# A weight-gradient matmul: slice 1 moved from the hardware queues to the casting queue, and a warm-up without a gap

## The chip, the cores and the metric

One core of a Trainium2 chip runs the kernel. The metric is the device time of one execution in microseconds (us). A time given for a kernel is the median of several executions. The granted TensorE clock was between 0.997 and 1.0 in all but two. Those two are executions of the kernel before, 179.28 and 179.5 us at a clock of 0.99, in two later series (e1 to e4 and e9 to e12); they stand almost 2 us above all its others and no cause is known. I compare medians. The ratios of those eight runs in the table below still contain them, which lowers these ratios by about 0.001 and widens their intervals.

## The reference

```python
# input (16, 512, 1024) f32, grad_output (16, 512, 768) f32
grad_weight = np.einsum('bmk,bmn->kn', input, grad_output)   # (1024, 768) f32
```

It is one matmul that contracts over 16 x 512 = 8192 rows. The kernel cuts them into 64 *slices* of 128 rows. A slice reads 128 x (1024 + 768) x 4 B = 0.92 MB.

## The kernel before

Each slice gives twelve 512-column bf16 matmuls in three *groups* of four: A (output rows 0 to 511, columns 0 to 511), B (output rows 512 to 1023, the same columns) and N (the other 256 columns, transposed). A group that is open holds four of the eight PSUM banks, so only two of the three can be open at once. `ORDER` says in which order the groups are worked off: `B12!` means "B, up to and with slice 11, then close", and closing adds the four banks to sums in SBUF, by VectorE. The queues of SyncE and ScalarE are called the hardware queues here, and that of GpSimd, which rounds f32 to bf16 on the way, the casting queue. In the cuts of code `...` stands for what is left out, and the comments are mine.

```python
ORDER = (
    "A1! N1 B2! N2 A2 N3! A3 B3 A4! B5 N5 B6! N7 A6 N8! A9! B10 N9 B12! N12! A12! "
    "B15 A15 AB16 A19! B19! N19! A22 B22 AB28 A31! B31! N31! A34 B34 AB47 A50! B50! N64!"
).split()
HW = 2
WARMUP = 9
...
# slices 0 and 1 in f32 over the queues of SyncE and ScalarE; other engines round them
nc.sync.dma_start(out=gf[0], in_=G[rows[0], 0:NA])
nc.scalar.dma_start(out=xf[0][:, 0:NA], in_=X[rows[0], 0:NA])
nc.sync.dma_start(out=gnf, in_=G[rows[0], NA:N])
nc.scalar.dma_start(out=xf[0][:, NA:K], in_=X[rows[0], NA:K])
nc.sync.dma_start(out=gf[1], in_=G[rows[1], 0:NA])
nc.scalar.dma_start(out=xf[1], in_=X[rows[1], :])
...
for i in range(WARMUP):
    nc.tensor.matmul(wps, ones, ones_wide, start=(i == 0), stop=(i == WARMUP - 1))
...
nc.gpsimd.dma_start(out=gn1, in_=G[rows[1], NA:N])
for s in range(HW, S):                      # 62 slices cast to bf16 by the transfer itself
    ...
    nc.gpsimd.dma_start(out=gt, in_=G[s * P : (s + 1) * P, :])
    nc.gpsimd.dma_start(out=xt, in_=X[s * P : (s + 1) * P, :])
```

After `ORDER`, slices 50 to 63 of A and B are worked off one output row block after the other, so that stores can start; this last stretch has a fixed length.

Of the kernel before, what the change touches and what calls it, by code (L numbers as in the profile page):

```python
# [8 lines left out]
P = 128  # L9
NA = 512  # L10
# [7 lines left out]
    "B15 A15 AB16 A19! B19! N19! A22 B22 AB28 A31! B31! N31! A34 B34 AB47 A50! B50! N64!"  # L18
).split()

HW = 2
WARMUP = 9
XBUFS = 42


# [1 line left out]
def kernel(  # L27
# [6 lines left out]
    nc = tc.nc  # L34
    bf16 = mybir.dt.bfloat16
    f32 = mybir.dt.float32

    B, M, K = input.shape
    _, _, N = grad_output.shape
    S = B * M // P  # L40
    KS = K // P
    NB = N - NA
# [3 lines left out]
    X = input.rearrange("b m k -> (b m) k")  # L46
    G = grad_output.rearrange("b m n -> (b m) n")
    OUT = out.rearrange("(ks p) n -> p ks n", p=P)

    head = ctx.enter_context(tc.tile_pool(name="head", bufs=1))  # L50
# [11 lines left out]
    xs = [None] * S  # L62
    gwide = [None] * S
    gnarrow = [None] * S
# [1 line left out]
    E = mybir.EngineType  # L66
    ctx.enter_context(tc.manual_schedule(engines={E.PE, E.DVE, E.Activation}))

    xf = [head.tile([P, K], f32, name=f"xf{s}") for s in range(HW)]
    gf = [head.tile([P, NA], f32, name=f"gf{s}") for s in range(HW)]  # L70
    gnf = head.tile([P, NB], f32, name="gnf")
    rows = [slice(s * P, (s + 1) * P) for s in range(HW)]
    nc.sync.dma_start(out=gf[0], in_=G[rows[0], 0:NA])
    nc.scalar.dma_start(out=xf[0][:, 0:NA], in_=X[rows[0], 0:NA])  # L74
    nc.sync.dma_start(out=gnf, in_=G[rows[0], NA:N])
    nc.scalar.dma_start(out=xf[0][:, NA:K], in_=X[rows[0], NA:K])  # L76
    nc.sync.dma_start(out=gf[1], in_=G[rows[1], 0:NA])
    nc.scalar.dma_start(out=xf[1], in_=X[rows[1], :])


    ones = nc.const_aps.tensor(1.0, (P, P), bf16)
    ones_wide = nc.const_aps.tensor(1.0, (P, NA), bf16)
    wps = psum.tile([P, NA], f32, name="bank7")
    for i in range(WARMUP):
        nc.tensor.matmul(wps, ones, ones_wide, start=(i == 0), stop=(i == WARMUP - 1))  # L85


    gn1 = head.tile([P, NB], bf16, name="gn1")
    nc.gpsimd.dma_start(out=gn1, in_=G[rows[1], NA:N])
    gnarrow[1] = gn1  # L90
    for s in range(HW, S):
        gt = xg.tile([P, N], bf16, name="gt")
        xt = xg.tile([P, K], bf16, name="xt")
        nc.gpsimd.dma_start(out=gt, in_=G[s * P : (s + 1) * P, :])  # L94
        nc.gpsimd.dma_start(out=xt, in_=X[s * P : (s + 1) * P, :])  # L95
        xs[s] = xt
        gwide[s] = gt[:, 0:NA]
        gnarrow[s] = gt[:, NA:N]

    QX = 256  # L100

    def round_pair(dst, src, c):
        nc.vector.tensor_copy(out=dst[:, c : c + QX], in_=src[:, c : c + QX])  # L103
        nc.scalar.copy(out=dst[:, c + QX : c + 2 * QX], in_=src[:, c + QX : c + 2 * QX])  # L104

    def round_slice(s):
        gt = head.tile([P, NA], bf16, name=f"g{s}")
        xt = head.tile([P, K], bf16, name=f"x{s}")
        round_pair(gt, gf[s], 0)

        for c in (0, NA) if s == 0 else (NA, 0):
            round_pair(xt, xf[s], c)
            if s == 0 and c == 0:
                gn0 = head.tile([P, NB], bf16, name="gn0")
                nc.vector.tensor_copy(out=gn0, in_=gnf)
                gnarrow[0] = gn0
        xs[s] = xt
        gwide[s] = gt

    def add_out(dst, src):  # L120
        nc.vector.tensor_add(out=dst, in0=src, in1=dst)  # L121

    def copy_out(dst, src, i):
        if i % 2 == 0:
            nc.vector.tensor_copy(out=dst, in_=src)  # L125
        else:
            nc.scalar.copy(out=dst, in_=src)  # L127

    def wide_mm(bank, k, s, start, stop, c0=0, c1=NA):
        nc.tensor.matmul(  # L130
            bank, xs[s][:, k * P : (k + 1) * P], gwide[s][:, c0:c1], start=start, stop=stop
        )
# [30 lines left out]
    def one_slice(part, close):  # L163
        s = part.done
        part.done += 1
        if s < HW and xs[s] is None:
            round_slice(s)
        opened = part.banks is None
        if opened:
            names = [free.pop(0) for _ in part.groups]  # L170
            part.banks = [(name, psum.tile([P, NA], f32, name=name)) for name in names]
        for i, (group, (name, bank)) in enumerate(zip(part.groups, part.banks)):
            part.matmul(bank, *group, s, opened, close)
            if close:
                dst = part.dst(*group)
                if part.first:
                    copy_out(dst, bank, i)
                else:
                    add_out(dst, bank)
                if part is parts["N"] and s == S - 1:  # L180
                    t, h = group
                    hb = NA // SQ
                    nc.vector.transpose(  # L183
                        out=turned[:, h * hb : (h + 1) * hb, :, t],
                        in_=dst.rearrange("p (b r) -> p b r", r=SQ),
                    )
                free.append(name)
        if close:
            part.banks = None
            part.first = False  # L190

    for step in ORDER:
        close = step.endswith("!")
        names = step.rstrip("!").rstrip("0123456789")
        upto = int(step.strip("ABN!"))
        while any(parts[n].done < upto for n in names):
            for n in names:
                if parts[n].done < upto:
                    one_slice(parts[n], close and parts[n].done == upto - 1)

    rows_of = out.rearrange("(b r) n -> r b n", r=SQ)
    for a in range(P // SQ):
        c = NA + a * NT * SQ
        nc.scalar.dma_start(
            out=rows_of[:, :, c : c + NT * SQ],
            in_=turned[a * SQ : (a + 1) * SQ].rearrange("p b r t -> p b (r t)"),
# [3 lines left out]
    for k in range(KS):  # L210
        slices = range(parts["A" if k < KS // 2 else "B"].done, S)
        pieces = [(0, NA)] if k < KS - 1 else [(0, 256), (256, 384), (384, NA)]
        for c0, c1 in pieces:
            name = free.pop(0)
            bank = psum.tile([P, NA], f32, name=name)[:, 0 : c1 - c0]
            for s in slices:
                wide_mm(bank, k, s, s == slices[0], s == slices[-1], c0, c1)
            add_out(acc[:, k, c0:c1], bank)
            free.append(name)
            W = NB if k < 4 else c1 - c0  # L220
            for c in range(c0, c1, W):
                nc.sync.dma_start(out=OUT[:, k, c : c + W], in_=acc[:, k, c : c + W])

# [29 lines left out]
```

## Time and profile before

| | kernel before |
|---|---|
| time | 177.08 us, 3 runs (176.94 to 177.35) |
| span in the profile | 175.2 us |
| TensorE busy | 171.0 us, 98% |
| DMA engines | full from about 4 to 144 us |
| matmuls | 768 of 512 columns at 0.216 us = 165.9 us, plus a slow start |

The prediction shows the page's busy rows, the pieces of the chain (the work that ended last, followed back from the last instruction; start, length, what) and the timeline of the start (start, busy time, engine, line, operation, count; in brackets the idle time before it and what ended it). Two more lines matter later. Here is one from the pieces of the chain (start, length, what):

```profile
35.02 14.73 PE bank L130 x68
```

And one from the timeline of the weight loads between 44 and 51 us (start, busy time, engine, line, operation, count; in brackets the idle time before it and what ended it):

```profile
46.13 3.13 PEld L130 LDWEIGHTS <-xt 128*128 128x128 bf16 x16 [0.38 <-DMA xt<-in_input_dram]
```

The first says that from 35.0 to 49.8 us TensorE works off A and B groups alone. The second says that at 46.13 us a weight load, which normally runs ahead of its matmul, had to wait for a slice that had only just landed. TensorE itself hardly stood still there: the matmul began 0.05 us late.

### The profile page before, as it was taken

How to read it: one execution, taken by the hardware profiler on the slowest of the kernel's cores; microseconds unless marked ns; L12 is line 12 of the kernel's file. 1: busy time of each engine (PE TensorE's matmuls, PEld its weight loads, DVE VectorE, ACT ScalarE, POOL GpSimd, SP SyncE). 2: the span in 40 equal slices, each digit the busy share in tenths (PEclk: the TensorE clock that was granted, in tenths of full speed). 3: DMA queues.
4: the chain of work that ended last, by engine and by line, in shares of the span. 5: the costliest groups of instructions: out<-in, count | busy, mean ns of one | idle time of the engine just before them, and what ended most of it. 6: DMA issues, size and time to landing. Idle time of an engine off the chain costs nothing.

```text
span 175.2 us, 1999 instructions
## 1 busy us (share of the span) xinstructions
PE 171.0 (98%) x805; PEld 77.8 (44%) x805; DVE 54.0 (31%) x91; ACT 6.8 (4%) x13; POOL 66.3 (38%) x129
## 2 busy tenths in 40 slices
PE   8999999999999999999999999999999999999993
PEld 2244444444444444444444444444444444444463
DVE  0665564790374100280320000047000003932122
ACT  3650000000000000000000000000000000000000
POOL 7344443444444444444444444444274200000000
PEclk9999999999999999999999999999999999999999
DMA  5999999999999999999999999999999990087513
GB/s 168 313 209 209 209 208 206 208 210 209 207 212 204 209 208 209 208 208 209 208 209 208 209 207 209 208 208 208 208 208 209 207 188 4 0 182 196 164 60 120
DMA packets 25048, 33.48 MB, mean 191 GB/s; under 512 B 6480, under 2 KB 16080, under 8 KB 25040
## 3 DMA queue, kind: packets, MB, share of 16 engines
q0 software_dynamic: 18000, 28.52, 89.0%
q1 hardware_dynamic: 2448, 2.75, 4.7%
q10 hardware_dynamic: 4592, 2.10, 4.6%
q8 instruction: 6, 0.10, 0.2%
q14 instruction: 2, 0.02, 0.0%
HBM read 58.72 MB, written 3.15 MB: 353 GB/s over the span
## 4 chain that ended last, share of the span: by engine, by line
PE 93%; DMA 4%; ACTq 0%; DVE 0%; issue 0%
PE bank L130 62%; PE bank L137 31%; DMA xf<-in_input_dram 4%; ACTq L76 0%; ACTq L74 0%; DVE x L103 0%; DVE acc L121 0%
## 5 line engine op out<-in xcount | busy, mean ns | idle before, releaser
L130 PE MATMUL bank<-gt,xt 128*128 128x512 bf16 (+2 forms) x524 | 108.7, 368 | 0.0
L130 PEld LDWEIGHTS <-xt 128*128 128x128 bf16 x524 | 50.0, 98 | 57.5 <-DMA xt<-in_input_dram 0.4
L121 DVE TENSOR_TENSOR acc<-bank,acc 128x512 f32<-128x512 f32 (+2 forms) x54 | 33.1, 664 | 71.7 <-PE bank L130 71.2
L137 PE MATMUL bank<-xt,gt 128*128 128x512 bf16 x248 | 55.0, 379 | 0.0
L95 POOL DMA_DIRECT2D xt<-in_input_dram x62 | 32.9, 530 | 36.1 <-DMA xt<-in_input_dram 35.4
L94 POOL DMA_DIRECT2D gt<-in_grad_output_dram x62 | 32.9, 531 | 33.9 <-DMA gt<-in_grad_output_dram 30.6
L137 PEld LDWEIGHTS <-gt 128*128 128x128 bf16 x248 | 24.3, 98 | 29.3
L121 DVE TENSOR_TENSOR acct<-bank,acct 128x512 f32<-128x512 f32 x20 | 12.6, 679 | 39.4 <-PE bank L137 39.3
L130 PE MATMUL bank<-g,x 128*128 128x512 bf16 x16 | 4.9, 438 | 0.6 <-DVE x L103 0.5
L85 PE MATMUL bank<-const-bfloat16-1.0 128*128 128x512 bf16 x9 | 4.0, 626 | 0.8 <-PEq L237 0.8
L130 PEld LDWEIGHTS <-x 128*128 128x128 bf16 x16 | 1.5, 106 | 3.8 <-DVE x L103 2.0
L183 DVE STREAM_TRANSPOSE turned<-acct 128x512 f32<-128x512 f32 x4 | 2.9, 714 | 0.1
L125 DVE COPY acc<-bank 128x512 f32<-128x512 f32 x4 | 2.7, 686 | 0.3 <-PE bank L130 0.3
L85 PEld LDWEIGHTS <-const-bfloat16-1.0 128*128 128x128 bf16 x9 | 1.2, 138 | 2.7 <-issue 2.7
L103 DVE CAST g<-gf 128x256 bf16<-128x256 f32 x2 | 0.6, 319 | 5.5 <-DMA gf<-in_grad_output_dram 5.5
L127 ACT COPY acc<-bank 128x512 f32<-128x512 f32 x4 | 2.2, 587 | 0.6 <-PE bank L130 0.5
L137 PE MATMUL bank<-x,gn 128*128 128x512 bf16 x8 | 2.1, 379 | 0.0
L125 DVE COPY acct<-bank 128x512 f32<-128x512 f32 x2 | 1.3, 686 | 1.3 <-PE bank L137 1.3
L104 ACT CAST x<-xf 128x256 bf16<-128x256 f32 x4 | 1.5, 402 | 0.5 <-DMA xf<-in_input_dram 0.5
L137 PEld LDWEIGHTS <-gn 128*128 128x128 bf16 x8 | 0.8, 105 | 1.2 <-issue 0.5
L104 ACT ACT_TABLE_LOAD x1 | 1.3, 1283 | 2.2 <-issue 2.2
L103 DVE CAST x<-xf 128x256 bf16<-128x256 f32 x4 | 1.1, 287 | 0.3 <-DMA xf<-in_input_dram 0.3
(8 smaller groups left out, 3.2 us busy)
## 6 DMA issues: line engine op xcount, KB each, us to landing
xt<-in_input_dram POOLq DMA_DIRECT2D x62, 256.0 KB, 8.5
gt<-in_grad_output_dram POOLq DMA_DIRECT2D x62, 192.0 KB, 8.5
out_dram<-acc SPq DMA_DIRECT2D x9, 128.0 KB, 2.9
out_dram<-turned ACTq DMA_DIRECT2D x4, 256.0 KB, 3.2
out_dram<-acc SPq DMA_DIRECT2D x3, 256.0 KB, 2.0
gf<-in_grad_output_dram SPq DMA_DIRECT2D x2, 256.0 KB, 5.1
xf<-in_input_dram ACTq DMA_DIRECT2D x2, 256.0 KB, 4.0
xf<-in_input_dram ACTq DMA_DIRECT2D x1, 512.0 KB, 6.9
```

The source lines that it names most:

```text
L85: nc.tensor.matmul(wps, ones, ones_wide, start=(i == 0), stop=(i == WARMUP - 1))
L94: nc.gpsimd.dma_start(out=gt, in_=G[s * P : (s + 1) * P, :])
L95: nc.gpsimd.dma_start(out=xt, in_=X[s * P : (s + 1) * P, :])
L103: nc.vector.tensor_copy(out=dst[:, c : c + QX], in_=src[:, c : c + QX])
L104: nc.scalar.copy(out=dst[:, c + QX : c + 2 * QX], in_=src[:, c + QX : c + 2 * QX])
L121: nc.vector.tensor_add(out=dst, in0=src, in1=dst)
L125: nc.vector.tensor_copy(out=dst, in_=src)
L127: nc.scalar.copy(out=dst, in_=src)
L130: nc.tensor.matmul(bank, xs[s][:, k * P : (k + 1) * P], gwide[s][:, c0:c1], start=start, stop=stop)
L137: nc.tensor.matmul(bank, gnarrow[s].rearrange("p (r t) -> p t r", t=NT)[:, t], xs[s][:, h * NA : (h + 1) * NA], start=start, stop=stop,)
L183: nc.vector.transpose(out=turned[:, h * hb : (h + 1) * hb, :, t], in_=dst.rearrange("p (b r) -> p b r", r=SQ),)
```

## The change

Its intent: give the hardware queues only slice 0, so that it is not followed by 0.79 MB of slice 1; let the casting queue of GpSimd round slice 1 on the way in, so that VectorE and ScalarE need not; keep TensorE's warm-up going until the data are there. Rows 4 and 5 of output blocks are also stored in two pieces instead of one. The diff is shortened; what stands in angle brackets, and the line of `round_pair`, are put together by me.

```diff
-HW = 2
-WARMUP = 9
+WARMUP = [512] * 9 + [128] * 3
...
-nc.sync.dma_start(out=gf[1], in_=G[rows[1], 0:NA])
-nc.scalar.dma_start(out=xf[1], in_=X[rows[1], :])
...
-for i in range(WARMUP):
-    nc.tensor.matmul(wps, ones, ones_wide, start=(i == 0), stop=(i == WARMUP - 1))
-gn1 = head.tile([P, NB], bf16, name="gn1")
-nc.gpsimd.dma_start(out=gn1, in_=G[rows[1], NA:N])
-for s in range(HW, S):
+for i, cols in enumerate(WARMUP):
+    nc.tensor.matmul(wps[:, 0:cols], ones, <ones, cols wide>, start=True, stop=True)
+for s in range(1, S):
     ... two GpSimd transfers per slice ...
...
-            round_slice(s)                  # casts of slices 0 and 1
+round_pair(g0, gf, 0); round_pair(xs[0], xf, 0); <cast of g0's narrow part>; round_pair(xs[0], xf, NA)
...
-            W = NB if k < 4 else c1 - c0
+            W = NB if k < 6 else c1 - c0
```

`ORDER` stays as it was.

More of the change, by code (lines that the diff above doesn't have):

```diff
@@ L67 @@
     ctx.enter_context(tc.manual_schedule(engines={E.PE, E.DVE, E.Activation}))
-    xf = [head.tile([P, K], f32, name=f"xf{s}") for s in range(HW)]
-    gf = [head.tile([P, NA], f32, name=f"gf{s}") for s in range(HW)]
-    gnf = head.tile([P, NB], f32, name="gnf")
-    rows = [slice(s * P, (s + 1) * P) for s in range(HW)]
-    nc.sync.dma_start(out=gf[0], in_=G[rows[0], 0:NA])
-    nc.scalar.dma_start(out=xf[0][:, 0:NA], in_=X[rows[0], 0:NA])
-    nc.sync.dma_start(out=gnf, in_=G[rows[0], NA:N])
-    nc.scalar.dma_start(out=xf[0][:, NA:K], in_=X[rows[0], NA:K])
-    nc.sync.dma_start(out=gf[1], in_=G[rows[1], 0:NA])
-    nc.scalar.dma_start(out=xf[1], in_=X[rows[1], :])
+    xf = head.tile([P, K], f32, name="xf")
+    gf = head.tile([P, N], f32, name="gf")
+    nc.sync.dma_start(out=gf[:, 0:NA], in_=G[0:P, 0:NA])
+    nc.scalar.dma_start(out=xf[:, 0:NA], in_=X[0:P, 0:NA])
+    nc.sync.dma_start(out=gf[:, NA:N], in_=G[0:P, NA:N])
+    nc.scalar.dma_start(out=xf[:, NA:K], in_=X[0:P, NA:K])
     ones = nc.const_aps.tensor(1.0, (P, P), bf16)
-    ones_wide = nc.const_aps.tensor(1.0, (P, NA), bf16)
     wps = psum.tile([P, NA], f32, name="bank7")
-    for i in range(WARMUP):
-        nc.tensor.matmul(wps, ones, ones_wide, start=(i == 0), stop=(i == WARMUP - 1))
-    gn1 = head.tile([P, NB], bf16, name="gn1")
-    nc.gpsimd.dma_start(out=gn1, in_=G[rows[1], NA:N])
-    gnarrow[1] = gn1
-    for s in range(HW, S):
+    for i, cols in enumerate(WARMUP):
+        nc.tensor.matmul(
+            wps[:, 0:cols],
+            ones,
+            nc.const_aps.tensor(1.0, (P, cols), bf16),
+            start=True,
+            stop=True,
+        )
+    for s in range(1, S):
         gt = xg.tile([P, N], bf16, name="gt")
@@ L98 @@
         gnarrow[s] = gt[:, NA:N]
+    xs[0] = head.tile([P, K], bf16, name="x0")
+    g0 = head.tile([P, N], bf16, name="g0")
+    gwide[0] = g0[:, 0:NA]
+    gnarrow[0] = g0[:, NA:N]
     QX = 256
@@ L104, in round_pair @@
         nc.scalar.copy(out=dst[:, c + QX : c + 2 * QX], in_=src[:, c + QX : c + 2 * QX])
-    def round_slice(s):
-        gt = head.tile([P, NA], bf16, name=f"g{s}")
-        xt = head.tile([P, K], bf16, name=f"x{s}")
-        round_pair(gt, gf[s], 0)
-        for c in (0, NA) if s == 0 else (NA, 0):
-            round_pair(xt, xf[s], c)
-            if s == 0 and c == 0:
-                gn0 = head.tile([P, NB], bf16, name="gn0")
-                nc.vector.tensor_copy(out=gn0, in_=gnf)
-                gnarrow[0] = gn0
-        xs[s] = xt
-        gwide[s] = gt
+    round_pair(g0, gf, 0)
+    round_pair(xs[0], xf, 0)
+    nc.vector.tensor_copy(out=g0[:, NA:N], in_=gf[:, NA:N])
+    round_pair(xs[0], xf, NA)
     def add_out(dst, src):
@@ L165, in one_slice @@
         part.done += 1
-        if s < HW and xs[s] is None:
-            round_slice(s)
         opened = part.banks is None
```

## The prediction

> **What bounds the kernel now.** I read the page's busy shares first, then the chain that ended last with its pieces in order of time, then the timeline of the first 12 us, since everything that the change touches but one store width lies there. The page:
>
> ```profile
> PE 171.0 (98%) x805; PEld 77.8 (44%) x805; DVE 54.0 (31%) x91; ACT 6.8 (4%) x13; POOL 66.3 (38%) x129
> ...
> DMA  5999999999999999999999999999999990087513
> GB/s 168 313 209 209 209 208 206 208 210 209 207 212 204 209 208 209 208 208 209 208 209 208 209 207 209 208 208 208 208 208 209 207 188 4 0 182 196 164 60 120
> ```
>
> TensorE is busy 98% of the span, and the DMA engines too are full, from the second slice to about 144 us. The pieces of the chain say where the matmuls stop being the limit:
>
> ```profile
> 1.67 6.91 DMA xf<-in_input_dram
> ...
> 8.60 0.31 DVE x L103
> ...
> 8.95 1.04 PE bank L130 x4
> 9.99 0.86 PE bank L137 x4
> 10.85 0.86 PE bank L130 x4
> ...
> 148.18 24.26 PE bank L130 x140
> 172.44 0.02 issue
> 172.46 0.29 DVE acc L121
> ```
>
> Four 512-column matmuls take 0.86 us, so one takes 0.216. There are 64 slices of 12 of them (768). Of these, 12 belong to slice 0 and come before 8.95 us; the other 756 need 756 x 0.216 = 163.3 us, and 8.95 + 163.3 = 172.2, against 172.44 in the chain. So from 8.95 us on TensorE never waits to speak of, and a gain there is out of reach for this change. What moves the end is only when slice 1's first matmul starts. In this trace a transfer sets that: the third input on the ScalarE queue (slice 1 of X, 512 KB), issued at 1.67 us, landed at 8.57, rounded by VectorE, then 8.95. The timeline shows what TensorE did meanwhile:
>
> ```profile
> 0.78 4.00 PE L85 MATMUL bank<-const-bfloat16-1.0 128*128 128x512 bf16 x9 [0.78 <-PEq L237]
> ...
> 4.91 1.82 PE L130 MATMUL bank<-g,x 128*128 128x512 bf16 x4
> ...
> 6.57 1.03 PE L137 MATMUL bank<-x,gn 128*128 128x512 bf16 x4
> ...
> 7.43 1.03 PE L130 MATMUL bank<-g,x 128*128 128x512 bf16 x4
> ...
> 8.95 1.04 PE L130 MATMUL bank<-g,x 128*128 128x512 bf16 x4 [0.49 <-DVE x L103]
> ```
>
> The groups are called A0, N0, B0 (slice 0) and B1 (slice 1). A0 starts at 4.91 and N0 at 6.57: 1.66 us for four, 0.415 each, so they run at half speed; from 6.57 on it is 0.216. B0 would let its successor start at 7.43 + 0.86 = 8.29, but B1 starts at 8.95. **0.66 us are lost to slice 1's arrival**, and 1.66 - 0.86 = 0.80 us to the slow A0, though today that second loss is hidden: without it TensorE would wait for slice 1 all the longer.
>
> **What the skill says.** "TensorE: Matmul & The Clock Gate", section "What's actually happening": the array runs at 1.2 instead of 2.4 GHz until a busy window of about 3.4 us has passed, and that window is free-running, so the moment differs from run to run. The trace agrees on the halves (0.415 against 0.216 us). The change of clock at 6.57 us lies 5.8 us after the first warm-up matmul, more than one window and less than two, which fits a free-running window. "DMA: Bandwidth & Descriptors", section "Issuing engines are not separate DMA queues": all queues interleave on the same 16 engines. This trace agrees: the DMA row is full at once. The same page, section "Latency and other measured facts", gives about 0.6 us to the first byte for the hardware path and about 1 us for the software path; here the trace's packet records are later: the first hardware packet at 1.76 us for an issue at 0.74, and the first packet of the GpSimd queue at 4.70 for an issue at 1.23. I use the trace's.
>
> **Part 1, slice 1 by the GpSimd queue.** It removes three issues (2 hardware transfers of 256 and 512 KB, 1 narrow piece on GpSimd of 64 KB) and six casts of slice 1 (VectorE 0.29 + 0.50 us, ScalarE 0.41 + 0.71), and with them the last step of the present chain, 8.57 to 8.95. It adds two GpSimd transfers (192 and 256 KB as written) at the head of that queue, at about 1.23 and 1.9 us; all later slices move back one place. The bytes read stay what they were: (768 + 1024) columns x 4 B x 128 rows = 0.92 MB for each of slices 0 and 1.
>
> When does slice 1 land? The steady GpSimd queue delivers 208 KB of bf16 per us, so a slice (448 KB) takes 2.15 us. Its first packets come at 4.70 us, as today's small narrow piece does. Slice 0's hardware data have their last packet at about 5.1 us and take most of the engines till then. So slice 1's packets run from about 5.0 to 7.2 us, and with about 0.4 us until completion shows (in the packet records the completion marks of one transfer spread over 0.4 us) it is there at **7.5 to 7.8 us, instead of the 8.57 to 8.95 of today**, and needs no cast.
>
> Slice 0's first pieces (256 KB on each hardware queue) are first in line in both kernels, so A0 stays at 4.9 us. Its casts are the same ones.
>
> What TensorE can do then: if the clock rises where it does now, A0 4.91, N0 6.57, B0 7.43, B1 at 8.29 without any wait, as slice 1 has been there for 0.5 us. **Gain 8.95 - 8.29 = 0.66 us.**
>
> **Part 2, the warm-up.** Nine matmuls at 0.427 us end at about 4.57 us, so 0.34 us stand empty before A0 at 4.91. Three of 128 columns at 0.427 / 4 = 0.107 us fill 0.32 of it. They end at 4.89, so they don't delay A0. Ending every warm-up matmul as its own group moves nothing. The gain, if any, is an earlier full clock. If the array were fast from A0 on, N0 would be at 5.77, B0 at 6.64 and B1 ready at 7.50, and it would then meet slice 1's landing at 7.5 to 7.8 and the copies that free B0's banks (four copies of 0.6 to 0.7 us on two engines after A0, the last done at about 7.2). So at most 8.95 - 7.7 = 1.25 us together with part 1. But the gap is 0.34 us of a window of 3.4, and in this trace the clock rose in the window that contains the gap. I think the gap did not hold it back and book 0 for it, but give a third or so of the weight to an earlier clock, since a free-running window also moves by luck. Before the change that luck was hidden behind the wait for slice 1; after it, it shows.
>
> **Part 3, the stores.** Rows 4 and 5 of the output go out as two pieces of 256 columns instead of one of 512: two more issues on SyncE, around 164 and 167 us. The last VectorE add is at 172.46 and its own store sets the end at 175.2. The DMA engines are far from full there. Booked at 0.
>
> **Sum.** 177.08 - 0.66 = 176.42 with the clock rising as now; about 175.8 with the earliest useful rise; about 177.0 with a late one (A0, N0 and part of B0 slow). I say 176.4.
>
> **Rivals.** (a) *Slice 1 arrives late*: the page gives a median of 8.5 us from issue to landing on the GpSimd queue, which from 1.23 and 1.9 would be 9.7 and 10.4, and B1 would start 1.5 us later than today, 178.5 us. Against it: those 8.5 us are queueing behind up to seven transfers, and slice 1 heads the queue; the narrow piece, now at its head, landed after 4.6 us. For it: between 5.5 and 6.0 us today's queue moves next to nothing after that piece, although the next transfer was issued; if that is a delay in making ready each transfer and not the hardware queues' traffic, slice 1 slips to about 8 us, which B1's 8.29 still covers. (b) *Starvation a little later*: TensorE is 0.66 us earlier, and the same slices must feed it. GpSimd's waits show slices 2 to 6 landing at latest at 10.22, 12.43, 14.64, 16.83 and 19.05 us, while TensorE takes each up 1.1 to 1.7 us later. Only around slice 11 (seen at 30.93, needed at about 31.4) is it 0.5 us, and those times lie some 0.3 to 0.6 us after the data, since GpSimd polls late. Also the queue itself should run 0.3 us or more ahead, as it isn't held up by hardware traffic till 8.3. A stall of 0.2 us at worst, then 176.6. (c) *The clock is the point*: full speed from A0, 175.8, as above. (d) *Nothing*: an arrival at just about 9 us gives 177.0.
>
> **Range and chances.** The whole lever is the stretch from 4.9 to 8.95 us, so no good case gains more than about 1.3 us, 0.7%, and 2% (3.5 us) faster is out of reach. A loss of 3.5 us would need slice 1 to land after 12 us. Range 175.7 to 177.0; faster 0.01, within 2% 0.975, slower 0.015.
>
> **What would show it.** Right: the wait of 0.49 us ahead of B1 gone, B1 at about 8.3 us, no gap before A0, A0 at about 4.9 still, the chain beginning with slice 0's input and then TensorE alone, and 163.3 + 0.2 us from B1 to the last matmul. Wrong in part 1: a wait on the GpSimd transfer ahead of B1, or idle TensorE between 10 and 32 us. Wrong in part 2: N0 earlier than about 6.4 us, or A0 later than 5.0. Wrong in part 3: the last add to the end of the span longer than today's 175.2 - 172.75 = 2.45 us.

## The result, and the profile after

The changed kernel takes 176.85 us (4 runs, 176.77 to 176.93) against 177.10 us before. The ratio is 0.9985 with a 95% interval of 0.9968 to 1.0002. Ratios are the mean time of one kernel's fast runs over that of the other's in the same rounds, so not quite the ratio of the medians. The time lies inside the predicted range, but I had forecast 0.68 us and 0.25 were measured, an amount that the interval doesn't separate from nothing.

The start went as predicted, and better. From the changed kernel's timeline (start, busy time, engine, line, operation, count):

```profile
0.78 4.32 PE L80 MATMUL bank<-const-bfloat16-1.0 128*128 128x512 bf16 x12 [0.78 <-PEq L228]
...
4.91 1.68 PE L123 MATMUL bank<-g,x 128*128 128x512 bf16 x4
...
6.42 1.03 PE L130 MATMUL bank<-x,g 128*128 128x512 bf16 x4
...
7.29 1.03 PE L123 MATMUL bank<-g,x 128*128 128x512 bf16 x4
...
8.15 1.03 PE L123 MATMUL bank<-gt,xt 128*128 128x512 bf16 x4
```

These are the warm-up, A0, N0, B0 and B1. A0 still starts at 4.91, nothing is waited for ahead of B1, and B1 starts at 8.15 us, where it started at 8.95. Yet the last VectorE add starts at 172.40 us against 172.46. So of 0.80 us won in the first 8 us, 0.06 arrive at the end. The pieces of the chain show where they go:

```profile
1.23 0.66 POOL gt L92
...
2.92 7.13 DMA xt<-in_input_dram
10.06 0.28 issue
10.35 8.53 DMA xt<-in_input_dram
...
37.48 8.54 DMA xt<-in_input_dram
46.02 0.05 issue
46.07 0.82 PE bank L123 x3
...
172.40 0.29 DVE acc L114
```

Before, the chain left the DMA queue at 8.57 us and was TensorE from there on. Now it is a transfer, the issue that this transfer's landing lets through, the next transfer, and so on, until 46.02 us. TensorE's timeline around that moment:

```profile
43.81 1.67 PE L123 MATMUL bank<-gt,xt 128*128 128x512 bf16 x7
46.07 3.63 PE L123 MATMUL bank<-gt,xt 128*128 128x512 bf16 x15 [0.58 <-DMA xt<-in_input_dram]
```

TensorE stands idle for 0.58 us as the page models the end of a matmul. By the starts of the two matmuls it is more: they lie 0.961 us apart where 0.216 is normal, so 0.745 us are lost. (About 15 matmul records are missing from this trace and make gaps of exactly two steps, 0.432 us, one after every 49; they are not waits.) The matmul that waits is the first of slice 18. Another 0.044 us are lost at slice 11, 0.79 us in all. The kernel before had lost 0.05 us at slice 18 itself, so 0.80 + 0.05 - 0.79 = 0.06 us arrive.

How does TensorE come to catch up with the data there? The queue lands a slice every 2.2 us (from the chain: 10.35 to 19.16 us for four slices). A slice with all three groups takes TensorE 12 x 0.216 = 2.59 us, so over the whole kernel TensorE falls behind the data. But in the stretch of 68 A and B matmuls it needs only 8 x 0.216 = 1.73 us per slice, as N is closed and has no banks. There it gains 0.47 us per slice on the data, on average. And at the end of the stretch, `A19! B19!` has A take slices 16, 17 and 18 before B takes any of them: a new slice is asked for every 4 x 0.216 = 0.86 us, which by this sum uses up 2 x (2.2 - 0.86) = 2.7 us of lead from slice 16 to slice 18. Slice 18 is the last slice that the stretch takes up. Before the change its data were there 0.05 us too late, after it 0.75.

The landing itself has not moved: slice 18's first matmul starts at 46.13 us before and 46.07 after. And nor has the beginning of the stream. GpSimd's issue that waits for slice 2's X, in the timelines of the kernels before and after:

```profile
10.22 0.53 POOL L95 DMA_DIRECT2D xt<-in_input_dram  x1 [0.64 <-DMA xt<-in_input_dram]
```

```profile
10.35 0.53 POOL L93 DMA_DIRECT2D xt<-in_input_dram  x1 [0.72 <-DMA xt<-in_input_dram]
```

Slice 1 was taken off the hardware queues and put in front of slice 2, and slice 2 came no earlier. All queues share engines that were full already, and the bytes are the same.

### The profile page after: what moved, and what is told of

It is laid out like the page before. It is cut to its first block, busy times and chain, and to the rows that moved or that the text cites. A ratio compares the mean times of both kernels' runs of the same rounds, so it can differ in the third digit from the quotient of the medians.

```text
span 175.2 us, 1984 instructions
## 1 busy us (share of the span) xinstructions
PE 170.2 (97%) x793; PEld 78.3 (45%) x808; DVE 53.4 (30%) x88; ACT 5.7 (3%) x10; POOL 66.9 (38%) x130
## 4 chain that ended last, share of the span: by engine, by line
PE 72%; DMA 24%; issue 1%; POOL 1%; DVE 0%; POOLq 0%
PE bank L123 46%; PE bank L130 26%; DMA xt<-in_input_dram 24%; POOL gt L92 1%; POOL xt L93 0%; DVE acc L114 0%; POOLq L228 0%
## 5 line engine op out<-in xcount | busy, mean ns | idle before, releaser
L123 PE MATMUL bank<-gt,xt 128*128 128x512 bf16 (+2 forms) x521 | 110.3, 368 | 1.2 <-DMA xt<-in_input_dram 0.6
L123 PEld LDWEIGHTS <-xt 128*128 128x128 bf16 x532 | 50.8, 98 | 59.2 <-DMA xt<-in_input_dram 1.4
L130 PE MATMUL bank<-xt,gt 128*128 128x512 bf16 x248 | 55.8, 379 | 0.2
L93 POOL DMA_DIRECT2D xt<-in_input_dram x63 | 33.5, 531 | 40.2 <-DMA xt<-in_input_dram 37.0
L80 PE MATMUL bank<-const-bfloat16-1.0 128*128 128x512 bf16 (+1 forms) x12 | 4.3, 547 | 0.8 <-PEq L228 0.8
L123 PE MATMUL bank<-g,x 128*128 128x512 bf16 x8 | 2.7, 475 | 0.0
L123 PEld LDWEIGHTS <-x 128*128 128x128 bf16 x8 | 0.8, 114 | 1.1 <-issue 0.6
L120 ACT COPY acct<-bank 128x512 f32<-128x512 f32 x2 | 1.1, 588 | 1.5 <-PE bank L130 1.5
L130 PE MATMUL bank<-x,g 128*128 128x512 bf16 x4 | 1.0, 379 | 0.0
L106 ACT CAST x<-xf 128x256 bf16<-128x256 f32 x2 | 0.8, 402 | 0.5 <-DMA xf<-in_input_dram 0.5
```

Source lines behind the costliest of these rows:

```text
L80: nc.tensor.matmul(wps[:, 0:cols], ones, nc.const_aps.tensor(1.0, (P, cols), bf16), start=True, stop=True,)
L106: nc.scalar.copy(out=dst[:, c + QX : c + 2 * QX], in_=src[:, c + QX : c + 2 * QX])
L120: nc.scalar.copy(out=dst, in_=src)
L123: nc.tensor.matmul(bank, xs[s][:, k * P : (k + 1) * P], gwide[s][:, c0:c1], start=start, stop=stop)
L130: nc.tensor.matmul(bank, gnarrow[s].rearrange("p (r t) -> p t r", t=NT)[:, t], xs[s][:, h * NA : (h + 1) * NA], start=start, stop=stop,)
```

## The experiments

My theory after the result, called *feed*: the start was improved by 0.8 us as planned; TensorE then meets slice 18, whose landing is fixed by the DMA engines' pace, and gives the gain back. Its rivals: the gain is lost elsewhere (the tail, the order's bank changes), or the start never set the end.

Each kernel ran with the kernel before on the same chip. "Before" is its median; a small order of groups is written as the part that differs.

| run | kernel | median, us | before | ratio, 95% interval |
|---|---|---|---|---|
| e1 | after, new order | 176.18 | 177.02 | 0.9938, 0.9900 to 0.9975 |
| e2 | before, new order | 176.80 | 177.02 | 0.9977, 0.9939 to 1.0015 |
| e3 | after, start held up | 176.88 | 177.02 | 0.9978, 0.9940 to 1.0015 |
| e4 | after, new order, start held up | 176.19 | 177.02 | 0.9937, 0.9895 to 0.9978 |
| e5 | after, new order, gap in the warm-up | 176.23 | 176.91 | 0.9961, 0.9949 to 0.9974 |
| e6 | after, new order, old stores | 176.27 | 176.91 | 0.9965, 0.9951 to 0.9978 |
| e7 | after, one slice not loaded (wrong result) | 175.84 | 176.91 | 0.9941, 0.9929 to 0.9954 |
| e8 | after, searched order | 175.96 | 176.91 | 0.9947, 0.9935 to 0.9960 |
| e9 | before, filled warm-up | 177.04 | 177.05 | 0.9986, 0.9941 to 1.0031 |
| e10 | after, gap in the warm-up | 177.03 | 177.05 | 0.9982, 0.9942 to 1.0022 |
| e11 | after, searched order, start held up | 176.07 | 177.05 | 0.9932, 0.9891 to 0.9973 |
| e12 | before, searched order | 176.87 | 177.05 | 0.9971, 0.9931 to 1.0011 |

### Use slice 18 later: e1 and e2

```diff
-B15 A15 AB16 A19! B19! N19! A22 B22 AB28
+B15 A15 AB16 A18! B19! N20! B22 AB28
```

The number of matmuls is the same. A now closes after slice 17, so slice 18 is first used by B, after B's slices 16 and 17: eight matmuls, or 1.73 us, later.

> The changed kernel with another order of groups around slice 18: A is closed after slice 17 instead of 18, N takes two more... slices 12 to 19 in one go, so slices 18 and 19 are first used later. Theory 'feed' (the 0.8 us won at the start are lost again because TensorE now catches up with slice 18, which lands at 46.0 us whatever TensorE did): no wait at 45 us any more, N's last group ends 0.75 us earlier, time 176.1 us (0.7 to 0.8 below the changed kernel's 176.85). Rival 'elsewhere' (the 0.8 us would be lost in the tail or at any other place, TensorE's end being set by something later than slice 18): a wait appears elsewhere and the time stays at 176.8.

Measured: 176.18 us, as *feed* said. The changed kernel with this order, TensorE around 46 us:

```profile
41.79 6.21 PE L123 MATMUL bank<-gt,xt 128*128 128x512 bf16 x28
47.84 3.40 PE L130 MATMUL bank<-xt,gt 128*128 128x512 bf16 x15
```

There is no wait. The last add starts at 171.56 us, 0.84 before the changed kernel's. Of this, 0.35 is an earlier start in this trace (B1 at 7.79 us instead of 8.15, the clock rose at 3.84), and the rest is less waiting: 0.31 us here, by the starts of the matmuls, against 0.79. But its chain still begins on the queue:

```profile
21.26 9.25 DMA xt<-in_input_dram
30.51 0.05 issue
30.56 1.04 PE bank L123 x4
```

Now slice 11 is the last slice that is waited for, and takes these 0.31 us. The bound has moved to the next place with little slack.

> The kernel before with the same new order. 'Feed': there TensorE waited only 0.05 us at slice 18, as its late start (B1 at 8.95 us) left it just behind the data, so the order alone is worth 0.05 to 0.1 us: 177.0. Rival 'the order is better by itself' (fewer or better placed bank changes): as fast as the changed kernel with that order, 176.1 to 176.4.

Measured: 176.80 us, against 177.02 for the kernel before, 0.2 below it where I had said at most 0.1, and far from the rival's 176.1 to 176.4. In its trace B1 starts at 8.76 us instead of 8.95, with nothing changed before it, and the last add at 172.21 instead of 172.46; so most of the excess in this trace is scatter in slice 1's arrival. The order is worth about 0.7 us to the changed kernel (176.85 to 176.18) and 0.2 to the kernel before. So it isn't better in itself: it lets an early start through. In the same order, the change is worth 176.80 - 176.18 = 0.62 us, close to the 0.66 that I had booked for part 1.

### Take the cause away, keep the order: e7

```diff
 for s in range(1, S):
+    if s == 5:
+        xs[s], gwide[s], gnarrow[s] = xs[4], gwide[4], gnarrow[4]
+        continue
```

> WRONG RESULT on purpose: the changed kernel in its own order, but slice 5 isn't loaded; its matmuls use slice 4's tiles. Same instructions on TensorE, 0.9 MB less read, so every slice from 6 on comes 2.2 us earlier. 'Feed': the wait at slice 18 is gone (slice 18 lands at about 43.8 us), as is the small one at slice 11, and the time is 176.0 to 176.2, as with the new order. Rival 'the order of groups itself costs 0.7 us (bank changes, weight loads), not the data': the wait stays and the time is 176.85.

Measured: 175.84 us (relative error of the output 0.18, as meant), a little faster than expected. The order is the changed kernel's own; the matmuls and closings are the same. TensorE around 46 us in this run:

```profile
41.69 6.85 PE L126 MATMUL bank<-gt,xt 128*128 128x512 bf16 x31
48.38 2.97 PE L133 MATMUL bank<-xt,gt 128*128 128x512 bf16 x13
```

The wait is gone with nothing changed but which slices are loaded, and so when the later ones arrive. With e1, which changed the order and not the data, this shows *feed* from both sides.

### Hold up the start: e3, e4, e11

```diff
-WARMUP = [512] * 9 + [128] * 3
+WARMUP = [512] * 9 + [128] * 9
```

> The changed kernel, its own order, with six more warm-up matmuls of 128 columns, which hold up slice 0's first matmul by 0.64 us (A0 at 5.55 instead of 4.91), less what a longer warm-up gives back in clock. 'Feed': the delay is taken out of the wait at slice 18, which shrinks from 0.75 to about 0.2 us; the time stays within 0.1 of 176.85. Rival 'the start sets the end': 177.4.

Measured: 176.88 us, no change. In this trace the clock happened to rise at 4.14 us, so A0 was not held up but started at 4.91 at full speed; B1 then waited for slice 1 until 8.08 us. The wait at slice 18 ended at 46.06 us, as in the other traces:

```profile
46.06 3.63 PE L123 MATMUL bank<-gt,xt 128*128 128x512 bf16 x16 [0.69 <-DMA xt<-in_input_dram]
```

By the starts it lost 0.85 us, more than the changed kernel's 0.745 and not the 0.2 that I had expected, as B1 came no later than there (8.08 us against 8.15). The time agrees with *feed*, but this one trace is not of the delay that I had wanted.

> The same six more warm-up matmuls in the changed kernel with the new order. 'Feed': with no wait left to hide it, the delay shows: 0.4 to 0.6 us slower than the new order without them, about 176.6 (A0 runs fully fast, so part of the 0.64 comes back). Rival 'the start sets nothing': 176.1 as without them.

Measured: 176.19 us, the same as without the extra warm-up: a miss. In its trace (of the slowest of its six executions, 176.49 us) A0 starts at 5.22 us, 0.3 later than the usual 4.91 and 0.5 later than in e1's, but at full speed, so B1 starts at 7.89 us, when slice 1 has landed, against 7.79 in e1's trace. And one slice near 24 us came late in this trace:

```profile
24.85 4.49 PE L123 MATMUL bank<-gt,xt 128*128 128x512 bf16 x20 [0.39 <-DMA xt<-in_input_dram]
```

So in e1's order the start is hidden too, part of the time: behind slice 1, and behind slices 8 to 11, by these two traces. I had taken "no wait at slice 18" for "no wait".

> The fastest kernel so far (searched order, 175.96) with six more warm-up matmuls, 0.64 us if the clock is slow then and 0.34 if it is fast; this repeats the test of the fourth run, which missed its forecast, in an order that hides less. If the start still sets the end: 0.1 to 0.35 us slower, 176.05 to 176.3, most where the clock rises late. If slice 1 (landing at 7.8 to 8.0 us) is what sets it in nearly every run: within 0.05 of 175.96.

Measured: 176.07 us (175.84 to 176.58) against 175.96 in e8: inside the first forecast, but 0.1 us is no more than the scatter. In its trace the clock rose late, at about 6.3 us by the spacing of the matmuls (there is no clock record); A0 started at 5.53 and B1 at 8.53, and that profiled run was one of the slower (176.51 us). B1 is 0.58 us later than in e8's trace, and so is the last add (171.97 against 171.39). In this pair the start sets the end in full; the medians don't show it.

### Part by part: e5, e6, e9, e10

e5 and e10 have the nine unfilled warm-up matmuls of before (`WARMUP = [512] * 9`), in e1's order and in the changed kernel's own. e9 puts the filled warm-up into the kernel before. e6 is e1 with `W = NB if k < 4`.

> The changed kernel with the new order of groups (slice 18 used later) but the warm-up of before: nine matmuls, with the gap of some 0.3 us ahead of A0. The new order is used because in it a later start is not hidden behind slice 18. Theory 'no gain from the gap' (the moment at which the clock rises differs by itself: 3.8 to 6.5 us in the six traces so far, with and without the gap): time within 0.15 us of the new order with the filled warm-up (176.18). Rival 'a gap delays the clock by up to a window': 0.3 to 0.8 us slower, 176.5 to 177.0, with the clock rising at 6 us or later in the trace.

Measured: 176.23 us, 0.05 above e1. The gap costs nothing that shows. But this order hides part of a late start: in its trace 0.38 us are lost at slice 11. The gap was not tested in the searched order, which hides less.

> Part 2 alone: the kernel before with the filled warm-up. Slice 1 still comes over the hardware queues and its first matmul starts at 8.8 to 8.95 us whatever the clock did before. Theory: no change, within 0.1 us of before. Rival (filling the gap has a worth of its own): 0.2 us or more faster.

Measured: 177.04 us against 177.05: nothing. In its trace the clock rose at 5.41 us, B0 was through earlier, and B1 waited the longer (0.78 us by the page, ended by the cast of slice 1, at 8.68 us).

> The changed kernel, its own order, with the unfilled warm-up of before (so part 1 with the store change). 'Feed': slice 18 sets the end, so again 176.85 within 0.1. Rival (the 0.15 to 0.25 us between the two kernels are the warm-up's): as slow as before.

Measured: 177.03 us against 177.05 for the kernel before, so 0.18 above what the changed kernel took. The forecast of 176.85 within 0.1 was missed by 0.08; the rival, "as slow as before", fits better by number. The trace speaks for *feed*, though: B1 starts at 7.86 us, over a microsecond ahead of before, and then

```profile
46.21 3.63 PE L123 MATMUL bank<-gt,xt 128*128 128x512 bf16 x15 [0.62 <-DMA xt<-in_input_dram]
```

Slice 18 landed 0.14 us later than in the changed kernel's trace, and the time follows it. So I can't tell the 0.0 to 0.25 us that the changed kernel and its near relatives gain (changed kernel, e3, e10) from scatter in the landing of slice 18, and don't ascribe it to the warm-up.

> The changed kernel with the new order and the stores of before (output rows 4 and 5 in one piece of 512 columns). Theory 'the stores do nothing': within 0.15 us of 176.18; from the last VectorE add to the end of the span 2.4 to 2.8 us as in both kernels. Rival: a part of the 0.25 us between the two kernels is the stores': 0.1 to 0.2 us slower.

Measured: 176.27 us against 176.18 in e1 and 176.23 for e5: the stores do nothing that shows. From the end of the last add to the end of the span it is 2.6 us in e6 and 2.5 in the kernels before and after.

### A version that uses the early start: e8 and e12

I wrote a small model of the feed from the traces (matmuls of 0.216 us, slices at their measured landing times, banks free 0.62 us after one another) and searched with it for an order in which no slice is waited for. What counts is the measured time of the order that it gave:

```diff
-A1! N1 B2! N2 A2 N3! A3 B3 A4! B5 N5 B6! N7 A6 N8! A9! B10 N9 B12! N12! A12!
-B15 A15 AB16 A19! B19! N19! A22 B22 AB28 A31! B31! N31! A34 B34 AB47 A50! B50! N64!
+A1! N1 B2! N2 A3 N4! A4! B4 B5 A5 B6! A7! N8! B9 N10! B11! A13! N15! A15 B15!
+A19! N17 B23! N22! B25! A28! A30! N26 N31! B34 B39! N39! B43! A50! B50! N64!
```

> The changed kernel with an order of groups that was searched with a model of this queue (matmuls of 0.216 us, slices landing at the times that the traces show, banks coming free 0.62 us after one another), so that no slice after the third is waited for even where the clock rises early. 'Feed' with the waits at slices 8 to 11 seen in two traces of the new order: gains where the clock rises early, 0.1 to 0.3 us below 176.18: 175.9 to 176.1. Rival: more changes of banks (more adds) cost TensorE something: 176.2 or more.

Measured: 175.96 us, the fastest correct kernel here, 0.95 below before and 0.12 above the kernel with a slice less to load. The head of its chain:

```profile
by line: PE bank L122 63.7%; PE bank L129 31.8%; PE bank L79 2.5%; DVE acc L113 0.2%; issue 0.0%
```

No transfer is in it any more: TensorE from its first warm-up matmul to the last. B1 and the last add in this run:

```profile
7.95 1.02 PE L122 MATMUL bank<-gt,xt 128*128 128x512 bf16 x4
...
171.39 0.29 DVE L113 TENSOR_TENSOR acc<-bank,acc 128x128 f32<-128x128 f32 x1 [0.49 <-PE bank L122]
```

> The kernel before with the searched order. This shows what parts 1 and 2 are worth where no later slice is waited for. 'Feed': the start of slice 1's matmuls at 8.8 to 8.95 us instead of 7.9 to 8.15 then shows in full: 176.6 to 176.8, 0.65 to 0.85 above the changed kernel with that order. Rival (the order is what gives the whole gain): 175.95 to 176.2.

Measured: 176.87 us, 0.18 below before, at the upper edge of the forecast and beyond it by 0.07. TensorE's start in this run:

```profile
4.92 1.71 PE L129 MATMUL bank<-g,x 128*128 128x512 bf16 x4
6.46 1.03 PE L136 MATMUL bank<-x,gn 128*128 128x512 bf16 x4
7.32 1.03 PE L129 MATMUL bank<-g,x 128*128 128x512 bf16 x4
8.77 1.04 PE L129 MATMUL bank<-g,x 128*128 128x512 bf16 x4 [0.42 <-DVE x L102]
```

It has the searched order and the old slice 1, and B1 at 8.77 us is what sets its end: no later slice is waited for, and its last add starts at 172.22 us, 0.83 after e8's, where B1 is 0.82 later. Where no later slice is waited for, the change is worth 0.95 - 0.18 = 0.77 us, by the gains over the kernel before.

One sum over all fourteen traces leaves no room for a loss elsewhere. Take the time from B1's start to the start of the last add, and subtract what is lost after B1 in waits for slices (the distance between two starts less 0.216 us; missing records left out). What is left is 163.44 to 163.48 us in every trace, in three orders, with either store and either warm-up, while B1 lies anywhere from 7.79 to 8.95 us and the waits from 0 to 1.21.

## Why the prediction was right or wrong, point by point

- **Right, the time and the class.** 176.85 lies in 175.7 to 177.0, and "within 2%" had nearly all the weight, because the lever ended at 8.95 us. But the number holds only because the range reached up to rival (d), "nothing"; the forecast gain of 0.66 us came through by 0.06 in the trace and 0.25 in the medians, so the mechanism failed after the start.
- **Right, part 1's start.** Slice 1 was there before B1 asked for it, A0 didn't move, the wait ahead of B1 was gone. In traces where TensorE asked for slice 1 sooner, it got it at 7.79 to 8.08 us (e1, e3), somewhat later than the 7.5 to 7.8 of the estimate (which also divided 448 KB of 1024 bytes by a rate in KB of 1000: a slice takes 2.2 us, not 2.15). B1 came at 8.15 us instead of the 8.29 foretold, since the clock rose at 6.23 us in this trace and at 6.53 in the one before. Where little or nothing later hides it (e1 with e2, e8 with e12), this is worth 0.62 to 0.77 us, around the 0.66 booked.
- **Wrong, the step from the start to the end.** "From 8.95 us on TensorE never waits to speak of [...] What moves the end is only when slice 1's first matmul starts." True of the kernel before, it doesn't follow for a kernel that starts earlier. TensorE had no slack left against slice 18, where it already waited 0.05 us, so whatever it was advanced by turned into a wait there: 0.745 us after the change. Two of the prediction's own signs show it: the chain was to be "TensorE alone" and stays with the casting queue until 46.02 us, and from B1 to the last matmul it was to be 163.5 us and is 164.2.
- **Wrong, rival (b) in its size.** I named starvation and put it at "a stall of 0.2 us at worst". I checked slices 2 to 6 and slice 11, up to 32 us. There I was right for the changed kernel's trace (0.044 us at slice 11; but 0.31 in e1's and 0.42 in e10's); the wait that mattered was 14 us further on. The signal was in the trace before: the weight load that waited 0.38 us at 46.13 us. The comparison that I made for slices 2 to 6 would have shown it too, as GpSimd's issue that waits for slice 18 starts only at 46.37 us, after TensorE's first use of the slice.
- **Wrong, "the queue itself should run 0.3 us or more ahead".** The engines were full in either kernel, and moving bytes from one queue to another doesn't give them time. Slice 2 was noticed at 10.35 us against 10.22.
- **Right, part 2 booked at 0**: e9 and e5 show none. Whether a gap can hold the clock up is still open: the clock rose at 4.57 to 6.53 us in the five traces with a gap (mean 5.67) and at 3.84 to 6.23 in eight without (mean 4.89; a ninth, e11's, has no record of it). So few values that lie so far apart don't settle it. If the clock rises only at the end of a window of 3.4 us, as the prediction has it, the gap held up none of these five: the latest rise, 6.53 us, puts the end of the window before it at 3.1 us, ahead of the gap. My remark that the luck of the clock "was hidden behind the wait for slice 1; after it, it shows" was wrong for the changed kernel, where slice 18 hides it instead.
- **Right, part 3 booked at 0** (e6).

## What to carry to other kernels

When an engine is always busy and its feed is also always full, the slack between them at every later step has to be worked out before an earlier start is called a gain: list when each input lands, list when it is first used, and take the smallest difference. A wait of the weight loads, 0.38 us where TensorE itself lost only 0.05, was the sign here that this difference was zero. And a gain that disappears so is not lost for good: changing the order in which the inputs are used, with the same work, brought it back here.

## What the Trainium skill lacked or had wrong

- "TensorE: Matmul & The Clock Gate", section "What you observe", has the clock rise around 4 us into matmul activity, give or take 0.5. In 13 traces here it rose 3.06 to 5.75 us after the first warm-up matmul at 0.78 us. The table in its section "What's actually happening" asks for at least one busy window, about 3.4 us of sustained activity; in e1's trace 3.06 us of matmuls were enough.
- "DMA: Bandwidth & Descriptors", section "Latency and other measured facts", gives about 1 us to the first byte for the software path. For the first GpSimd transfer of the changed kernel 3.4 us passed from the start of its issue (1.23 us) to its first packet (4.63 us in the packet records). The engines were moving slice 0 for the hardware queues from 1.75 us on, so how much of it is the software path is not shown.
- No place that I found in that page says whether a casting transfer goes at the pace of the bytes it reads or of those it writes. Here f32 to bf16 wrote 208 GB/s, so it read 416; and it was not slower, by bytes read, than the plain f32 transfers, for slice 2 landed at the same time whichever queue brought slice 1.
- "Runtime: NRT & Kernel Launch", to which the point belongs, speaks of instruction fetches but not of what one does to a busy stream of data. The changed kernel's packet records have one of 16 KB from 24.10 to 24.99 us, and just after it GpSimd sees a slice 3.0 us after the last one instead of 2.2 (its wait is 1.56 us where 0.72 is usual). In e4's trace such a late slice was waited for. That the one causes the other was not tested, and it is doubtful: the same trace has such packets at 51.92 and 79.44 us, where slices come at most 2.3 us apart.
